# Two attention heads in the halves of the rows, four column blocks in the modulation, a copy before the norm

## The chip, the cores and the metric

The kernel runs on one core of a Trainium2 chip. The metric is the time of one execution in microseconds of the device, lower is better; the median of several runs is given. The core has five instruction streams: PE (TensorE, matmuls; its weight loads are a row of their own, PEld), DVE (VectorE), ACT (ScalarE), POOL (GpSimd) and SP (SyncE, which here only issues DMAs). Each works its instructions off in program order.

## The reference, cut to what matters

One even layer (mLSTM heads beside a Hyena channel group) and one odd layer (neighbourhood attention), each followed by an MLP; 1024 latent tokens, 256 context tokens, model width 1024, all in float32. Two parts of it matter here. Every layer first makes six vectors out of the conditioning vector, one for the latent tokens and one for the context tokens:

```python
mod_x = (silu_c @ w_mod[l] + b_mod[l])        # w_mod[l]: 1024 x 6144
mod_c = silu_cc @ w_mod[l] + b_mod[l]
```

And the odd layer's attention, 16 heads of width 64, where each latent query sees a window of 8 rows by 16 columns of the 16 x 64 token grid and all 256 context keys in one softmax:

```python
q = rms_norm(p[:, :, 0], qn) * NA_HD ** -0.5
k = rms_norm(p[:, :, 1], kn)
s_lat = jnp.einsum('bhqd,bhkd->bhqk', q_r, k_blk) + bias
s_ctx = jnp.einsum('bhqd,bhkd->bhqk', q_r, kc)
p = jax.nn.softmax(jnp.concatenate([s_lat, s_ctx], axis=-1), axis=-1)
out = p[..., :nk] @ v_blk + p[..., nk:] @ vc
```

## The kernel before

**Stages.** The program makes the Hyena filters (to some 230 us of the profile), the Hyena group (to 600), the mLSTM heads with the output projection (to 960), the first layer's MLP (to some 2000), the attention of the odd layer (2007 to 2650), its output projection and the second MLP. A scheduling layer sets each engine's order when the program is built: instructions have priorities (`pr`), work is taken in that order as its inputs and buffers come free, and what results is a fixed order for each engine.

**Matmuls in float32.** Where exactness matters, an operand is split into a high part of type F32R and the rest (`split`, L110: ACT casts, DVE or POOL subtracts, L112 and L113), and a product is the sum of three F32R matmuls: high by high, high by low, low by high (`gemm`, L177 to L179). An F32R matmul is one instruction in the profile. A plain F32 matmul is two, which are called passes here.

**The modulation** (`mod_steps`, L208). A third of a layer's w_mod (2048 columns) is worked off in 16 steps: a step loads 128 rows by 1024 columns (512 KB) into a tile `wm` and multiplies it by the conditioning vectors. The weights of the matmul are only 32 columns wide, so its output goes to one of four blocks of 32 partitions of one bank: step (k, jj) writes blocks 2jj and 2jj+1 with 512 columns each (L218). The first third of layer 0 is made at the start with three `wm` tiles (bank `psq`), the other two thirds during the mLSTM stage, up to four steps behind each load that `wload` makes (L162, bank `psn`), and the three of layer 1 during the first MLP, four steps for each pair of weight blocks, with a single `wm` tile (L296, bank `psm`): there a step's DMA is issued only when the matmuls of the step before it have read the tile.

**The attention** (`natten_proj`, L890; `natten_attn`, L946) works two heads at a time, eight times. The projection makes q and k of both heads in 128 rows (64 each), each group of up to 512 tokens in a bank `psg`, and normalises them from there: ACT squares the bank (L901), PE sums over each head's 64 rows (L903), ACT and DVE make the inverse root, and DVE multiplies the bank by it (L912, L914). Then the q of each head is written twice by ACT: `Q[hh]` holds the high part of head hh in both halves of its 128 rows (four 64-row copies per group, L933) and `Ql[hh]` the low part in one half and zeros in the other (L934, POOL clears it). `Kt[hh]` holds the high part of the head's k in one half and its low part in the other (L939, L940). So one matmul over 128 rows gives high by high plus high by low, and a second one, with `Ql`, low by high. For each of four blocks of query columns (cb), each head (hh) and each of two row blocks (rb) these two matmuls are made against the 256 context keys (into `pc`) and against a window of 384 keys (into `p_`), L979 and L980. Then come the row maximum (L983, L985), the exponentials (L990, L991), the scaling (L995), transposes on PE (L1000, L1007) that ACT and DVE copy out (L1002, L1009), and the products with the values (L1015, L1019), in which the two heads' outputs go to the two halves of the 128 partitions.

**Banks.** PSUM has eight banks, shared out by tag: `psum(**PS3)` (g=3, f=3, m=1, n=1) holds from the mLSTM stage to the end. The attention takes its projections from `g`, its scores and outputs from `f`, all transposes from `m`, the norm's sum from `n`. `PS2` is defined and not used.

Of the kernel before, what the change touches and what calls it, by code (L numbers as in the profile page):

```python
# [17 lines left out]
P = 128  # L18
# [9 lines left out]
def kernel(ctx: ExitStack, tc: tile.TileContext, A, out):  # L28
# [38 lines left out]
    PS2 = dict(g=3, f=3, m=1, q=1)  # L67
# [33 lines left out]
    def sub(o, a, b):  # L101
        return tt(o, a, b, ALU.subtract)
# [105 lines left out]
    def mod_steps(l, g, pool, bufs, tag):  # L208

        ps = [None]  # L210
        for i in range(16):
            def step(k=i // 2, jj=i % 2):
                if k == 0 and jj == 0:
                    ps[0] = pt([P, 512], tag)
                w = mk(pool, [P, 8, P], bufs[0], bufs[1]).rearrange("p a b -> p (a b)")
                nc.sync.dma_start(w, A["w_mod"][l, k * P:(k + 1) * P, g * 2048 + jj * 1024:g * 2048 + (jj + 1) * 1024])
                for j in (2 * jj, 2 * jj + 1):
                    T.matmul(ps[0][32 * j:32 * j + 32, :], sil[:, k, :], w[:, (j - 2 * jj) * 512:(j - 2 * jj + 1) * 512],  # L218
                             start=(k == 0), stop=(k == 7))
                if k == 7 and jj == 1:  # L220
                    mod_end(l, g, ps[0], tag)
            yield step
# [667 lines left out]
    def natten_proj(hp, h, ap_, nl, cst, order=((0, 0), (0, 1), (1, 0), (1, 1), (1, 2), (2, 0), (2, 1), (2, 2))):  # L890

        with pr("np"):
            bd, gain = cst

            Q = [mk(nl, [P, LAT], "Q", 4, F32R) for _ in range(2)]
            Ql = [mk(nl, [P, LAT], "Ql", 3, F32R) for _ in range(2)]
            for hh in range(2):
                G.memset(Ql[hh][64 - 64 * hh:128 - 64 * hh].bitcast(F32), 0.0)
            def normed(ps, n, sc):
# [20 lines left out]
            for j, g in order:  # L920
                t0, n = GR[g]
                if j not in w:
                    w[j] = wload("qkv" if hp else "q0", A["w_qkv"][3 * hp + j], E4 if hp == 0 else None, into=(nl, ("Q", "Q"), 4) if hp == 0 and j == WQ else None)
                ts = slice(t0, t0 + n)
                ps = gemm(w[j], h, g, n)
                if j == 0:
                    r = normed(ps, n, gain)
                    blkd = lambda x: x.rearrange("p (c r q) -> p c r q", c=4, q=16)
                    rv = r.rearrange("p (r c q) -> p c r q", c=4, q=16)
                    for hh in range(2):  # L930
                        a = slice(64 * hh, 64 * hh + 64)
                        for b in (0, 64):
                            S.copy(blkd(Q[hh][b:b + 64, ts]), rv[a])  # L933
                        sub(blkd(Ql[hh][a, ts]), rv[a], blkd(Q[hh][a, ts]).bitcast(F32))  # L934
                elif j == 1:
                    r = normed(ps, n, None)
                    for hh in range(2):
                        a, b = slice(64 * hh, 64 * hh + 64), slice(64 - 64 * hh, 128 - 64 * hh)
                        S.copy(Kt[hh][a, ts], r[a, :n])  # L939
                        sub(Kt[hh][b, ts], r[a, :n], Kt[hh][a, ts].bitcast(F32))  # L940
                else:
                    with pr("v0" if hp == 0 else None):
                        S.copy(vT[:, ts], ps[:, :n])
            return Q, Ql, Kt, vT

    def natten_attn(hp, qkv, ap_, nl, store):  # L946
        with pr("na"):
            Q, Ql, Kt, vT = qkv
# [12 lines left out]
            for cb in range(4):  # L961
# [4 lines left out]
                pT = []  # L966
                for hh in range(2):
                    TM = mk(nl, [P, 2, 384], "TM", 2)
                    nc.gpsimd.dma_start(TM, A["rpbT"][2 * hp + hh, ct])
                    kl = Kt[hh][:, 0:LAT].rearrange("p (r c) -> p r c", c=64)  # L970
                    pc = pt([P, 2, CTX], "f")
                    st = mk(ap_, [P, 8], "st", 6)
                    pw, pe = [], []
                    for rb in range(2):
                        c0 = rb * 512 + cb * P
                        p_ = pt([P, 512], "f")
                        for o, kx in ((pc[:, rb], Kt[hh][:, LAT:NT]),
                                      (p_[:, :384], kl[:, 4 * rb:4 * rb + 12, KC0[cb]:KC0[cb] + 32])):
                            T.matmul(o, Q[hh][:, c0:c0 + P], kx, start=True, stop=False)  # L979
                            T.matmul(o, Ql[hh][:, c0:c0 + P], kx, start=False, stop=True)  # L980
                        pw.append(p_)
                        pe.append(mk(ap_, [P, 640], "pe", 4))
                    V.tensor_reduce(out=st[:, 0:2], in_=pc, axis=AX.X, op=ALU.max)  # L983
                    for rb in range(2):
                        V.tensor_tensor_reduce(out=pe[rb][:, 0:384], in0=pw[rb][:, :384], in1=TM[:, rb], scale=1.0, scalar=st[:, rb:rb + 1],  # L985
                                               op0=ALU.add, op1=ALU.max, accum_out=st[:, 2 + rb:3 + rb])
# [198 lines left out]

    with tc.tile_pool(name="nl", bufs=1, reuse_waits="tile") as nl, \
# [29 lines left out]
        for d in range(8):  # L1216
            w = wload("ow1", A["w_o"][d][:, 0:7], E5, (0, 7))
            residual(xg, 1, 0, d, 0, gemm(w, h2, 0, 512, ks=range(7)), 512)
    with tc.tile_pool(name="xg1", bufs=1, reuse_waits="tile", side="right") as xp:
# [149 lines left out]
```

## Time and profile before

| | us |
|---|---|
| median of 3 runs | 3432.65 (3432.45 to 3433.51) |
| the profiled execution's own time | 3440.28 |
| its span, first to last instruction | 3438.5 |
| PE busy | 3288.0 |
| DVE busy | 2055.2 |
| ACT busy | 1209.4 |
| POOL busy | 350.3 |

All microseconds in what follows come from this one profiled execution, whose time lies 7.6 us (0.2%) above the median of the runs. A row of the timeline has a start, a length, the engine, the line, output<-inputs and a count; for PE the shape `128*64 128x512` means 128 rows by 64 columns of weights and 512 moving columns. The length of a matmul contains a tail that overlaps the next one: what a matmul costs PE is the distance to the next start.

### The profile page before, as it was taken

How to read it: one execution, taken by the hardware profiler on the slowest of the kernel's cores; microseconds unless marked ns; L12 is line 12 of the kernel's file. 1: busy time of each engine (PE TensorE's matmuls, PEld its weight loads, DVE VectorE, ACT ScalarE, POOL GpSimd, SP SyncE). 2: the span in 40 equal slices, each digit the busy share in tenths (PEclk: the TensorE clock that was granted, in tenths of full speed). 3: DMA queues.
4: the chain of work that ended last, by engine and by line, in shares of the span. 5: the costliest groups of instructions: out<-in, count | busy, mean ns of one | idle time of the engine just before them, and what ended most of it. 6: DMA issues, size and time to landing. Idle time of an engine off the chain costs nothing.

```text
span 3438.5 us, 44541 instructions
## 1 busy us (share of the span) xinstructions
PE 3288.0 (96%) x17660; PEld 2647.1 (77%) x17660; DVE 2055.2 (60%) x3655; ACT 1209.4 (35%) x2554; POOL 350.3 (10%) x295
## 2 busy tenths in 40 slices
PE   6889979999999999999999999999999899999999
PEld 3777878677877878787788867777777688888887
DVE  4858978356576544444454676666676654545444
ACT  5742222244343121111212376666665421121211
POOL 1331222101121000000000121111110200000000
PEclk9999989999999999999999999999999999999999
DMA  6432221775632121222211112222225211111111
GB/s 202 156 108 67 79 63 58 239 230 198 209 131 81 55 92 56 82 66 68 68 36 45 68 54 67 68 68 67 62 70 169 74 50 49 48 45 49 49 49 68
DMA packets 104011, 306.07 MB, mean 89 GB/s; under 512 B 12497, under 2 KB 24905, under 8 KB 102394
## 3 DMA queue, kind: packets, MB, share of 16 engines
q1 hardware_dynamic: 94154, 266.60, 23.6%
q0 software_dynamic: 6464, 28.84, 2.8%
q10 hardware_dynamic: 3184, 7.78, 0.7%
q8 instruction: 139, 2.28, 0.3%
q14 instruction: 70, 0.57, 0.1%
HBM read 255.93 MB, written 43.05 MB: 87 GB/s over the span
## 4 chain that ended last, share of the span: by engine, by line
PE 76%; DVE 12%; DMA 5%; ACT 3%; POOL 3%; issue 2%; SPq 0%; ACTq 0%; DVEq 0%; POOLq 0%
PE psg L178 12%; PE psg L179 12%; PE psg L177 12%; PE psf L313 7%; PE psf L314 7%; PE psf L315 7%; DMA wm<-in_w_mod 2%; DVE b L96 2%; PE psf L1015 2%; DVE n L108 2%; PE psm L1000 1%; DVE q L96 1%; PE psm L218 1%; PE psf L979 1%; PE psf L980 1%
## 5 line engine op out<-in xcount | busy, mean ns | idle before, releaser
L177 PE MATMUL psg<-h,wh 128*128 128x512 f32 (+1 forms) x2728 | 1017.7, 373 | 20.0 <-ACT wh L112 9.4
L178 PE MATMUL psg<-h,wh 128*128 128x512 f32 (+1 forms) x2728 | 1017.1, 373 | 4.1 <-DVE h L108 2.8
L179 PE MATMUL psg<-h,wl 128*128 128x512 f32 (+1 forms) x2728 | 1008.8, 370 | 10.1 <-DVE wl L113 5.0
L177 PEld LDWEIGHTS psg<-h,wh 128*128 128x128 f32 x2728 | 519.4, 190 | 121.1 <-issue 22.2
L178 PEld LDWEIGHTS psg<-h,wh 128*128 128x128 f32 x2728 | 519.7, 191 | 120.6 <-issue 33.8
L179 PEld LDWEIGHTS psg<-h,wl 128*128 128x128 f32 x2728 | 519.0, 190 | 107.5 <-issue 17.3
L108 DVE SCALAR_TENSOR_TENSOR x<-psf,modT,x 128x512 f32<-128x512 f32 (+1 forms) x512 | 347.4, 683 | 223.0 <-PE psf L315 222.7
L314 PE MATMUL psf<-al,w2h 128*128 128x512 f32 (+1 forms) x1280 | 472.1, 369 | 0.5 <-DVE al L113 0.5
L315 PE MATMUL psf<-ah,w2l 128*128 128x512 f32 (+1 forms) x1280 | 471.5, 368 | 0.0
L313 PE MATMUL psf<-ah,w2h 128*128 128x512 f32 (+1 forms) x1280 | 469.5, 369 | 1.2 <-ACT ah L112 0.8
L112 ACT CAST w2h<-w2r 128x1024 fp32r<-128x1024 f32 x64 | 67.2, 1051 | 767.6 <-PE psf L314 596.0
L313 PEld LDWEIGHTS psf<-ah,w2h 128*128 128x128 f32 x1280 | 240.7, 189 | 45.4 <-ACT ah L112 3.8
L314 PEld LDWEIGHTS psf<-al,w2h 128*128 128x128 f32 x1280 | 241.6, 189 | 42.9 <-DVE al L113 1.8
L315 PEld LDWEIGHTS psf<-ah,w2l 128*128 128x128 f32 x1280 | 241.5, 189 | 41.2 <-issue 1.3
L112 ACT CAST wh<-wr 128x1024 fp32r<-128x1024 f32 (+2 forms) x144 | 148.5, 1031 | 292.7 <-PE psg L178 228.2
L113 DVE TENSOR_TENSOR wl<-wr,wh 128x1024 fp32r<-128x1024 f32 (+1 forms) x105 | 127.6, 1216 | 151.7 <-ACT wh L112 151.1
L108 DVE SCALAR_TENSOR_TENSOR rr<-psg,rr 128x512 f32<-128x512 f32 x160 | 101.4, 634 | 191.0 <-ACT rr L302 190.9
L113 POOL TENSOR_TENSOR wl<-wr,wh 128x1024 fp32r<-128x1024 f32 (+1 forms) x39 | 128.3, 3289 | 623.5 <-ACT wh L112 602.6
L113 DVE TENSOR_TENSOR w2l<-w2r,w2h 128x1024 fp32r<-128x1024 f32 x64 | 78.2, 1223 | 154.4 <-ACT w2h L112 152.6
L302 ACT ACTIVATE rr<-psg 128x512 f32<-128x512 f32 x160 | 88.1, 551 | 212.5 <-PE psg L179 211.1
L112 ACT CAST ah<-rr 128x512 fp32r<-128x512 f32 x160 | 92.3, 578 | 164.1 <-DVE rr L108 164.1
L113 DVE TENSOR_TENSOR al<-rr,ah 128x512 fp32r<-128x512 f32 x160 | 101.8, 636 | 77.6 <-ACT ah L112 77.6
(294 smaller groups left out, 4353.5 us busy)
## 6 DMA issues: line engine op xcount, KB each, us to landing
wm<-in_w_mod SPq DMA_DIRECT2D x96, 512.0 KB
wr<-in_w SPq DMA_DIRECT2D x64, 512.0 KB
w2r<-in_w SPq DMA_DIRECT2D x64, 512.0 KB
big<-d SPq DMA_DIRECT2D x39, 640.0 KB
TM<-in_rpbT POOLq DMA_DIRECT2D x64, 384.0 KB, 3.4
wr<-in_w_in SPq DMA_DIRECT2D x29, 512.0 KB
wr<-in_w_qkv SPq DMA_DIRECT2D x24, 512.0 KB
d<-b SPq DMA_DIRECT2D x8, 1280.0 KB
```

Of the source, the lines that this page charges most:

```text
L96: return (e or V).tensor_tensor(out=o, in0=a, in1=b, op=op)
L108: return V.scalar_tensor_tensor(out=o, in0=a, scalar=s, in1=b, op0=op0, op1=op1)
L112: S.copy(hi, x)
L113: (e or V).tensor_tensor(out=lo, in0=x, in1=hi.bitcast(F32), op=ALU.subtract)
L177: T.matmul(ps[:M, :n], hi[:, k, :M], hh[g][:, k, :n], start=(i == 0), stop=False)
L178: T.matmul(ps[:M, :n], hi[:, k, :M], hl[g][:, k, :n], start=False, stop=False)
L179: T.matmul(ps[:M, :n], lo[:, k, :M], hh[g][:, k, :n], start=False, stop=(i == len(ks) - 1))
L302: S.activation(r[:, :n], ps[:, :n], AF.Relu)
L313: T.matmul(ps[:, :n], w2h[:, d], ah[g], start=(i == 0), stop=False)
L314: T.matmul(ps[:, :n], w2h[:, d], al[g], start=False, stop=False)
L315: T.matmul(ps[:, :n], w2l[:, d], ah[g], start=False, stop=(i == 1))
L1015: T.matmul(po[64 * hh:64 * hh + 64, rb], Vw[:, rb + j, 64 * hh:64 * hh + 64], pT[hh][0][rb][:, j], start=(j == 0), stop=False)
```

## The change

Three parts, and the numbers of tiles and banks that go with them.

**Scores.** `Q[0]` and `Kt[0]` now hold the high parts of both heads, `Q[1]` and `Kt[1]` the low parts: one `split` for each group in place of the copies by halves, and no `Ql`. The three products of a head are matmuls over its own 64 rows, written alternately for head 0 (rows 0 to 63 of the array) and head 1 (rows 64 to 127), each head into a bank of its own. Both heads' scores are now made before either head's softmax.

**Projection.** Before the norm of q and k, ACT copies the bank into a tile `qs`; the square and the last multiplication read the copy.

**Modulation.** A step now loads 256 of each of four 512-column blocks (128 rows by 4 runs of 1 KB instead of one run of 4 KB), and writes all four blocks of 32 partitions with 256 columns each. The 16 steps go through the eight k for the first 256 columns, then for the second 256.

**Banks.** `PS2` becomes g=2, f=4, m=1, n=1 and holds during the attention; `PS3` is set again behind it. `TM` has three tiles instead of two, `pe` six instead of four.

```diff
-    PS2 = dict(g=3, f=3, m=1, q=1)
+    PS2 = dict(g=2, f=4, m=1, n=1)
...
-            def step(k=i // 2, jj=i % 2):
-                if k == 0 and jj == 0:
+            def step(k=i % 8, c0=i // 8 * 256):
+                if k == 0 and c0 == 0:
                     ps[0] = pt([P, 512], tag)
-                w = mk(pool, [P, 8, P], bufs[0], bufs[1]).rearrange("p a b -> p (a b)")
-                nc.sync.dma_start(w, A["w_mod"][l, k * P:(k + 1) * P, g * 2048 + jj * 1024:g * 2048 + (jj + 1) * 1024])
-                for j in (2 * jj, 2 * jj + 1):
-                    T.matmul(ps[0][32 * j:32 * j + 32, :], sil[:, k, :], w[:, (j - 2 * jj) * 512:(j - 2 * jj + 1) * 512],
-                             start=(k == 0), stop=(k == 7))
+                w = mk(pool, [P, 8, P], bufs[0], bufs[1]).rearrange("p (j a) b -> p j (a b)", j=4)
+                nc.sync.dma_start(w, A["w_mod"][l, k * P:(k + 1) * P, g * 2048:(g + 1) * 2048].rearrange("p (j c) -> p j c", j=4)[:, :, c0:c0 + 256])
+                for j in range(4):
+                    T.matmul(ps[0][32 * j:32 * j + 32, c0:c0 + 256], sil[:, k, :], w[:, j], start=(k == 0), stop=(k == 7))
...
-            def normed(ps, n, sc):
+            def normed(pj, n, sc):
+                ps = mk(nl, [P, 512], "qs", 2)
+                S.copy(ps[:, :n], pj[:, :n])
...
-                    for hh in range(2):
-                        a = slice(64 * hh, 64 * hh + 64)
-                        for b in (0, 64):
-                            S.copy(blkd(Q[hh][b:b + 64, ts]), rv[a])
-                        sub(blkd(Ql[hh][a, ts]), rv[a], blkd(Q[hh][a, ts]).bitcast(F32))
+                    split(blkd(Q[0][:, ts]), blkd(Q[1][:, ts]), rv)
...
-                    for hh in range(2):
-                        a, b = slice(64 * hh, 64 * hh + 64), slice(64 - 64 * hh, 128 - 64 * hh)
-                        S.copy(Kt[hh][a, ts], r[a, :n])
-                        sub(Kt[hh][b, ts], r[a, :n], Kt[hh][a, ts].bitcast(F32))
+                    split(Kt[0][:, ts], Kt[1][:, ts], r[:, :n])
...
-                            T.matmul(o, Q[hh][:, c0:c0 + P], kx, start=True, stop=False)
-                            T.matmul(o, Ql[hh][:, c0:c0 + P], kx, start=False, stop=True)
...
+                def scores(outs, rb, cols):
+
+                    c0 = rb * 512 + cb * P
+                    for i, (x, y) in enumerate(((0, 0), (0, 1), (1, 0))):
+                        for hh in range(2):
+                            T.matmul(outs[hh], Q[x][HD[hh], c0:c0 + P], cols(Kt[y])[HD[hh]], start=(i == 0), stop=(i == 2))
...
+    psum(**PS2)
     with tc.tile_pool(name="nl", bufs=1, reuse_waits="tile") as nl, \
...
+    psum(**PS3)
     with tc.tile_pool(name="xg1", bufs=1, reuse_waits="tile", side="right") as xp:
```

The order on PE in the attention, before: one column block of one of the last heads. `psg` rows are the projection of the next pair of heads, `psm` the transposes, `KK` and `Q`, `Ql` the scores.

```order
L1000 MATMUL psm_17837<-ident,pe_17818 128x128 x3
L1015 MATMUL psf_17897<-s_3172_17835,Vw_17801 64x128
L979 MATMUL psf_17932<-KK_17349,Q_17343 128x256
L980 MATMUL psf_17932<-KK_17349,Ql_17345 128x256
L979 MATMUL psf_17932<-KK_17349,Q_17343 128x256
L980 MATMUL psf_17932<-KK_17349,Ql_17345 128x256
L177 MATMUL psg_18234<-h_1652_8689,wh_18186 128x512
L178 MATMUL psg_18234<-h_1653_8690,wh_18186 128x512
L1007 MATMUL psm_17843<-ident,pe_17812 128x128 x2
L1007 MATMUL psm_17843<-ident,pe_17818 128x128 x2
L979 MATMUL psf_17934<-KK_17349,Q_17343 128x384
L980 MATMUL psf_17934<-KK_17349,Ql_17345 128x384
```

The scores stand among projections and transposes, all of which use the whole array. The same place in the changed program, the context keys first (`psf_18192` is head 0, `psf_18193` head 1; `KK_17589` and `Q_17587` are the high parts):

```order
L1015 MATMUL psf_18149<-s_3188_18106,Vw_18045 64x128
L971 MATMUL psf_18192<-KK_17589,Q_17587 128x256
L971 MATMUL psf_18193<-KK_17589,Q_17587 128x256
L971 MATMUL psf_18192<-KK_17590,Q_17587 128x256
L971 MATMUL psf_18193<-KK_17590,Q_17587 128x256
L971 MATMUL psf_18192<-KK_17589,Q_17588 128x256
L971 MATMUL psf_18193<-KK_17589,Q_17588 128x256
L1007 MATMUL psm_18114<-ident,pe_18050 128x128 x2
L1007 MATMUL psm_18114<-ident,pe_18051 128x128 x2
L971 MATMUL psf_18192<-KK_17589,Q_17587 128x256
```

and a few rows on, the window keys of the first row block (`psf_18208` is head 0, `psf_18209` head 1):

```order
L971 MATMUL psf_18208<-KK_17589,Q_17587 128x384
L1000 MATMUL psm_18130<-ident,pe_18055 128x128 x3
L971 MATMUL psf_18208<-KK_17590,Q_17587 128x384
L971 MATMUL psf_18208<-KK_17589,Q_17588 128x384
L900 MATMUL psn_18483<-n_3273_18481,bd_8340 128x512
L1000 MATMUL psm_18136<-ident,pe_18056 128x128 x3
L1015 MATMUL psf_18149<-s_3194_18134,Vw_18045 64x128
```

For the context keys the two heads alternate, as written. For these window keys they don't: head 0's three matmuls come first, with transposes among them, and head 1's three only after the next products with the values. Over the whole attention 542 of the 768 score matmuls stand next to one of the other head, and 226 do not, 215 of them 384 wide.

The modulation on PE in the first MLP, one step among the projections (`psg`), before:

```order
L179 MATMUL psg_10008<-h_1543_8262,wl_9999 128x512
L177 MATMUL psg_10008<-h_1543_8262,wh_9998 128x512
L218 MATMUL psm_8695<-wm_9972,sil 32x512 x2
L178 MATMUL psg_10008<-h_1544_8263,wh_9998 128x512
L179 MATMUL psg_10008<-h_1543_8262,wl_9999 128x512
```

and in the changed program:

```order
L179 MATMUL psg_13617<-h_1543_8358,wl_13608 128x512
L177 MATMUL psg_13617<-h_1543_8358,wh_13607 128x512
L218 MATMUL psm_12272<-wm_13575,sil 32x256 x4
L178 MATMUL psg_13617<-h_1544_8359,wh_13607 128x512
L179 MATMUL psg_13617<-h_1543_8358,wl_13608 128x512
```

Each step has four narrower matmuls in the place of two, and in the first MLP the same 16 projection matmuls stand between the steps of a group of four as before. In the mLSTM stage the 32 steps make 37 blocks among other work instead of 34, since seven of them are split, one matmul here and three a little later.

More of the change, by code (lines that the diff above doesn't have):

```diff
@@ L895, in natten_proj @@
             Q = [mk(nl, [P, LAT], "Q", 4, F32R) for _ in range(2)]
-            Ql = [mk(nl, [P, LAT], "Ql", 3, F32R) for _ in range(2)]
-            for hh in range(2):
-                G.memset(Ql[hh][64 - 64 * hh:128 - 64 * hh].bitcast(F32), 0.0)
-            def normed(ps, n, sc):
+            def normed(pj, n, sc):
+                ps = mk(nl, [P, 512], "qs", 2)
+                S.copy(ps[:, :n], pj[:, :n])
                 sq = n2()
@@ L943, in natten_proj @@
                         S.copy(vT[:, ts], ps[:, :n])
-            return Q, Ql, Kt, vT
+            return Q, Kt, vT
     def natten_attn(hp, qkv, ap_, nl, store):
         with pr("na"):
-            Q, Ql, Kt, vT = qkv
+            Q, Kt, vT = qkv
             vl = vT[:, 0:LAT].rearrange("p (r c) -> p r c", c=64)
@@ L966, in natten_attn @@
                 pT = []
+                HD = [slice(64 * hh, 64 * hh + 64) for hh in range(2)]
+                TMs, sts, pes = [], [], []
                 for hh in range(2):
-                    TM = mk(nl, [P, 2, 384], "TM", 2)
+                    TM = mk(nl, [P, 2, 384], "TM", 3)
                     nc.gpsimd.dma_start(TM, A["rpbT"][2 * hp + hh, ct])
-                    kl = Kt[hh][:, 0:LAT].rearrange("p (r c) -> p r c", c=64)
-                    pc = pt([P, 2, CTX], "f")
-                    st = mk(ap_, [P, 8], "st", 6)
@@ L973, in natten_attn @@
[L973 to L986, printed above, removed]
+                    TMs.append(TM)
+                    sts.append(mk(ap_, [P, 8], "st", 6))
+                    pes.append([mk(ap_, [P, 640], "pe", 6) for _ in range(2)])
@@ new lines, in scores @@
+                def scores(outs, rb, cols):
[3 more added lines that the diff above has]
+                            T.matmul(outs[hh], Q[x][HD[hh], c0:c0 + P], cols(Kt[y])[HD[hh]], start=(i == 0), stop=(i == 2))
+                pcs = [pt([P, 2, CTX], "f") for _ in range(2)]
+                for rb in range(2):
+                    scores([x[:, rb] for x in pcs], rb, lambda k: k[:, LAT:NT])
@@ new lines, in natten_attn @@
+                for hh in range(2):
+                    V.tensor_reduce(out=sts[hh][:, 0:2], in_=pcs[hh], axis=AX.X, op=ALU.max)
+                for rb in range(2):
+                    pw = [pt([P, 512], "f") for _ in range(2)]
+                    scores([x[:, :384] for x in pw], rb,
+                           lambda k: k[:, 0:LAT].rearrange("p (r c) -> p r c", c=64)[:, 4 * rb:4 * rb + 12, KC0[cb]:KC0[cb] + 32])
+                    for hh in range(2):
+                        V.tensor_tensor_reduce(out=pes[hh][rb][:, 0:384], in0=pw[hh][:, :384], in1=TMs[hh][:, rb], scale=1.0,
+                                               scalar=sts[hh][:, rb:rb + 1], op0=ALU.add, op1=ALU.max, accum_out=sts[hh][:, 2 + rb:3 + rb])
@@ L987, in natten_attn @@
+                for hh in range(2):
+                    st, pe, pc = sts[hh], pes[hh], pcs[hh]
                     V.tensor_scalar(out=st[:, 2:4], in0=st[:, 2:4], scalar1=-1.0, scalar2=None, op0=ALU.mult)
```

3 lines of the change are left out of this document (1 added, 2 removed).

## The prediction

> **What bounds the kernel now.** First the page: its totals and the engines of the chain that ended last.
>
> ```profile
> span 3438.5 us, 44541 instructions
> PE 3288.0 (96%) x17660; PEld 2647.1 (77%) x17660; DVE 2055.2 (60%) x3655; ACT 1209.4 (35%) x2554; POOL 350.3 (10%) x295
> PE 76%; DVE 12%; DMA 5%; ACT 3%; POOL 3%; issue 2%; SPq 0%; ACTq 0%; DVEq 0%; POOLq 0%
> ```
>
> PE is nearly always busy and carries 76% of the chain. So I ask of each edit what it does to the distance from one matmul's start to the next. The windows of the four stages that it touches (columns: window, length, busy of PE, PEld, DVE, ACT, POOL, granted clock, DMA share, GB/s): the start, the mLSTM stage, the first MLP, the attention.
>
> ```profile
> 0.00:55.00 55.00, 31.42 (x104) 8.09 (x104) 16.60 (x40) 20.44 (x40) 1.63 (x9) 0.88 0.75 247
> 600.00:800.00 200.00, 192.75 (x1052) 137.94 (x1052) 90.45 (x216) 67.20 (x200) 19.62 (x8) 0.98 0.69 228
> 1050.00:1710.00 660.00, 655.81 (x3333) 521.22 (x3332) 304.99 (x463) 122.63 (x193) 3.50 (x4) 1.00 0.24 74
> 2007.00:2650.00 643.00, 630.47 (x4147) 493.05 (x4147) 447.36 (x998) 424.15 (x1051) 88.25 (x134) 0.99 0.25 76
> ```
>
> PE stands still for 7.3 of 200, 4.2 of 660 and 12.5 of 643 us in the last three; work taken from PE there, or given to it, shows in the time. At the start PE idles 23.6 of 55 us and the DMAs move 247 GB/s.
>
> **The modulation.** One step in the first MLP, with the projections around it, and two steps of the mLSTM stage which the scheduler had torn apart:
>
> ```profile
> 1088.04 1.05 PE L218 MATMUL psm<-wm,sil 128*32 128x512 f32 x4
> 1089.03 0.50 PE L178 MATMUL psg<-h,wh 128*128 128x512 f32 x1
> 1089.36 0.40 PE L179 MATMUL psg<-h,wl 128*128 128x512 f32 x1
> 1089.60 0.39 PE L177 MATMUL psg<-h,wh 128*128 128x512 f32 x1
> ...
> 1092.56 0.39 PE L178 MATMUL psg<-h,wh 128*128 128x512 f32 x1
> 1093.06 1.05 PE L218 MATMUL psm<-wm,sil 128*32 128x512 f32 x4
> ```
>
> ```profile
> 646.93 1.04 PE L218 MATMUL psn<-wm,sil 128*32 128x512 f32 x2
> 647.90 0.66 PE L785 MATMUL psm<-ident,big 128*128 128x128 f32 x4
> 648.49 1.06 PE L218 MATMUL psn<-wm,sil 128*32 128x512 f32 x6
> 649.48 0.50 PE L178 MATMUL psg<-h,wh 128*128 128x512 f32 x1
> ```
>
> A block of two instructions (one matmul) holds PE for 0.97 us (646.93 to 647.90), one of four (two matmuls, a whole step) 0.99 (1088.04 to 1089.03), one of six 0.99 (648.49 to 649.48). So matmuls for different blocks of 32 partitions run side by side, three at least, and a block costs its two passes whatever its width in blocks. Four at once is what the change needs; I take it as given. Within the block of two, the second starts 0.45 us after the first (the row lasts 1.04, one instruction 0.59, by the least in the next rows). A pass over 512 columns so costs at most 0.45, and half the columns save some 0.21 of each: 0.99 becomes 0.57, a gain of 0.42 for each step.
>
> ```profile
> L218 PE MATMUL psm<-wm,sil x192: 592/605/617, 1050.9 to 1700.8; 128*32 128x512 f32 x192
> L218 PE MATMUL psn<-wm,sil x128: 592/617/1062, 615.3 to 797.7; 128*32 128x512 f32 x128
> L218 PE MATMUL psq<-wm,sil x64: 592/825/1063, 11.3 to 48.4; 128*32 128x512 f32 x64
> 1089.14 3.88 DMA wm<-in_w_mod
> 2664.86 3.86 DMA wr<-in_w_o
> ```
>
> At four instructions a step these are 48, 32 and 16 steps (the last two rows are of the chain of waits: start, length, DMA). First MLP: 48 x 0.42 = 20.2 us. But there the next step's DMA is issued only once the tile is read (1089.14), lands 3.88 us later, and PE arrives about then: 1092.56 to 1093.06 is 0.50 where 0.23 is usual (1089.36 to 1089.60). Both the DMA's issue and PE's return move forward by the same amount, so the wait only grows if the load takes longer in runs of 1 KB. The nearest row is the load of 2664.86, 512 KB in runs of 512 bytes: 3.86 us, no longer. I take 0.1 us for 36 of the 48 steps (three in each four follow closely), 3.6 us, with ends of 0 and 0.3 (11 us). That leaves 16.6. mLSTM stage: 32 x 0.42 = 13.4, less two or three blocks more than before at 0.57 (torn steps) and the 7.3 us in which PE waits anyway: 10, with ends of 6 and 13. Start: matmuls at 825 against 605 ns, three tiles in turn, so each round of load and matmul gets shorter by part of a step, and the loads have more pieces: 3, with ends of -3 and 6. Sum: 29.6 us less.
>
> **The scores.** One stretch of the attention:
>
> ```profile
> L1015 PE MATMUL psf<-s,Vw x768: 272/273/476, 2048.2 to 2651.6; 128*64 128x128 f32 x192
> 2151.20 0.55 PE L1000 MATMUL psm<-ident,pe 128*128 128x128 f32 x3 [0.19 <-ACT s L1002]
> 2151.68 0.43 PE L1015 MATMUL psf<-s,Vw 128*64 128x128 f32 x2
> 2152.05 0.39 PE L979 MATMUL psf<-KK,Q 128*128 128x256 f32 x1
> 2152.27 0.28 PE L980 MATMUL psf<-KK,Ql 128*128 128x256 f32 x1
> 2152.39 0.28 PE L979 MATMUL psf<-KK,Q 128*128 128x256 f32 x1
> 2152.51 0.28 PE L980 MATMUL psf<-KK,Ql 128*128 128x256 f32 x1
> ...
> 2153.09 0.60 PE L1007 MATMUL psm<-ident,pe 128*128 128x128 f32 x4
> ...
> 2153.71 0.34 PE L980 MATMUL psf<-KK,Ql 128*128 128x384 f32 x1
> 2153.89 0.40 PE L178 MATMUL psg<-h,wh 128*128 128x512 f32 x1
> ```
>
> A score matmul costs 0.12 us at 256 columns (2152.39 to 2152.51) and 0.18 at 384 (2153.71 to 2153.89). Before there are 256 of each: 30.7 + 46.1 = 76.8 us. The change has 384 of each, with 64 rows. If two heads that stand next to each other run side by side, the 256-wide ones take some 192 slots and the 384-wide ones, 169 in pairs and 215 alone by the order, some 300: 23.0 + 54.0 = 77.0. So even then the matmuls gain nothing: the three products cost in halves what two cost in full, and torn pairs eat the rest. If none run side by side it is 115.2, 38 us more.
>
> Then there is the price of changing the array's partition. L1015 and L1019 use it in halves of columns. The row of three L1000 starts its last at 2151.48 (0.55 less 0.27, the length of one); L1015 follows 0.20 later where 128 columns take 0.11 (four L1007 in 0.60), and its second pass 0.16 later (0.43 less 0.27): 0.14 us lost on entering. It then leaves at 2152.05, 0.21 after that second pass, and the next start is 0.22 on where 0.12 is usual: 0.20 lost. By the order there are 192 such changes before and 476 after, counted from the last modulation step to the end, since almost each short run of half-row matmuls stands between full ones: 284 more. The bounds are 0.10 each (only the drain, where the weights of the next would wait for a semaphore anyway) and 0.17 (half of 0.34): 28 and 48 us. I take the middle, 0.13: 37 us. The nearest row with halves of rows is one from the gates, F32 and without a partner:
>
> ```profile
> 235.63 0.28 PE L178 MATMUL psg<-h,wh 128*128 128x256 f32 x1
> 235.86 1.10 PE L675 MATMUL psg<-s,q 64*100 64x512 f32 x2
> ```
>
> It starts 0.23 after a matmul that takes 0.12: 0.11 lost on entering. The Trainium skill, TensorEngine Tiling, section Tiling Modes, speaks against this change with the same rule: "Changing tiling mode (not just tile) drains the TensorE". It gives no price; by it all 284 changes cost, as in the sum.
>
> **The copy, the casts, the banks.**
>
> ```profile
> L933 ACT CAST Q<-n 64x512 fp32r<-64x512 f32 x64 | 39.5, 618 | 0.8
> L957 ACT COPY Vw<-psm 128x512 f32<-128x512 f32 x32 | 18.6, 582 | 7.3 <-PE psm L955 7.3
> L96 DVE TENSOR_TENSOR Ql<-n,Q 64x512 fp32r<-64x512 f32 x32 | 21.8, 681 | 2.9 <-ACT Q L933 2.5
> L96 DVE TENSOR_TENSOR KK<-n,KK 64x512 fp32r<-64x512 f32 x32 | 22.0, 686 | 1.9 <-ACT KK L939 0.9
> ```
>
> For a q group ACT drops from four casts to one and gains a copy (0.58, by the copy of the same size): 16 groups x (3 x 0.62 - 0.58) = 20 us less; for k one cast goes and the copy comes, even. DVE loses half of its 64-row subtractions: 22 us. ACT and DVE have idle time in this stage (424 and 447 of 643), so this buys time only by ending PE's waits sooner. The copy lies ahead of the square and lengthens the norm's chain by 0.58 for a pair of heads' group; projections for the next pair run a whole pair ahead, which hides it; if that cover were gone it would be 40 x 0.58 = 23 us. Two `g` banks instead of three suffice if the copy comes within a gemm's length (24 matmuls x 0.23 = 5.5 us). PE's idle 12.5 us shrink when PE itself becomes slower, its helpers lighter and `f` deeper: I take 10 off, with ends of 0 and 12.5. POOL no longer clears `Ql`; nothing waits for that.
>
> **The sum.** Modulation -29.6, score matmuls 0, changes of partition +37, waits -10: -2.6 us. Against its own time of 3440.28 the profiled execution would come to 3437.7; against the median of 3432.65, which lies 7.6 below, 3430. A difference under 0.2% (6.9 us, 3425.8 to 3439.5) is about what a measurement of this kernel cannot tell from none. With its bounds this case reaches from 3412 (changes at 0.10, full gains) to 3455 (0.17, waits kept, late loads).
>
> **The rivals.**
>
> *Free changes.* Matmuls in F32R may enter and leave a part of the array without a drain. For it speaks the only F32R row with half an array:
>
> ```profile
> 231.23 0.28 PE L178 MATMUL psg<-h,wh 128*128 128x256 f32 x1
> 231.35 1.09 PE L671 MATMUL psg<-h,wh 128*64 128x512 f32 x4
> ```
>
> 64 columns of weights after 128, and it starts 0.12 us later, as always. Against it: that matmul has no partner in the other half, so it may not use a divided array at all. The 284 changes then cost nothing: -29.6 - 10 = -40, 3393. Chance 0.17.
>
> *Free, but one after the other.* If F32R matmuls don't divide the array, halves don't overlap either: +38, no changes, -10 of waits, -29.6: -2, 3431. Chance 0.13.
>
> *One after the other, and each change paid*: slower. No row shows two F32R matmuls side by side; the pairs that are seen to overlap are F32. Then +38 + 37 - 12 - 29.6 = +33, 3466. It decides as soon as fewer than a third of the pairs overlap. Against it: the column blocks overlap so cleanly. The Trainium skill, TensorE: Matmul & The Clock Gate, Part 3, says that matmuls in different row groups run concurrently, measured 3.07 times faster for four; no run here shows it, and by it the score matmuls cost the 77 us of the sum. Chance 0.13.
>
> *Late modulation loads.* Four times as many pieces take 0.6 us longer in 36 steps: +18 against the forecast, 3448. Against it stands the 3.86 us of 512-byte runs. Chance 0.07.
>
> **How the numbers follow.** The forecast's case has 0.50, the rivals 0.17, 0.13, 0.13, 0.07. Range 3393 to 3462: it takes in the forecast's case, the second and fourth rival and about half of each of the others, so some 0.15 is left out. Faster by over 0.2%: 0.17 from the first rival, 0.17 of the forecast's 0.50, 0.05 of the second: 0.39. Slower: 0.15 of the forecast's, 0.13, 0.06, 0.02: 0.36. Within: 0.25.
>
> **What would show it.** In the profile after, a modulation block should hold PE for 0.57 us, with PE's wait ahead of it in the MLP up by 0.1. Two score matmuls of different heads should start within hundredths of a microsecond, with the next pair 0.12 or 0.18 on. The first matmul after a run of half rows should come 0.1 late, and the one after it 0.1 more. The window from the first to the second MLP should be some 27 us longer, the first MLP 17 shorter. The forecast is wrong if L971 enters without delay (then 3393), if pairs start a slot apart (then 3466), or if blocks of four still hold PE for 0.9 us (then +25).

## The result, and the profile after

The changed kernel takes 3477.38 us (median of 4 runs, 3475.41 to 3479.45) against 3433.08 for the kernel before (4 runs, 3432.45 to 3436.87): 44 us or 1.2% slower, ratio 1.0123 with an interval of 1.011 to 1.0136. The forecast was 3430, the range ended at 3462. The two profiled executions took 3479.45 and 3440.28 us, 39.2 apart, which is what has to be explained below.

The page of the changed kernel: totals, and the engines of the chain that ended last.

```profile
span 3477.7 us, 45667 instructions
PE 3305.4 (95%) x18300; PEld 2656.4 (76%) x18300; DVE 2030.0 (58%) x3615; ACT 1189.5 (34%) x2523; POOL 340.6 (10%) x279
PE 64%; DVE 4%; DMA 3%; ACT 2%; issue 1%; POOL 1%; SPq 0%; ACTq 0%; DVEq 0%; POOLq 0%
```

DVE and ACT are busy for 25 and 20 us less and the program is 39 us longer: as in the kernel before, PE sets the time. So the question is again where the distance between the starts of PE's matmuls grew.

**Before the attention the change gains.** One modulation step of the first MLP (the projections around it are L177 to L179), and two groups of L218 (in each row the last two times are the first and the last start of the group):

```profile
1080.02 0.39 PE L177 MATMUL psg<-h,wh 128*128 128x512 f32 x1
1080.70 0.64 PE L218 MATMUL psm<-wm,sil 128*32 128x256 f32 x8 [0.29 <-DMA wm<-in_w_mod]
1081.27 0.50 PE L178 MATMUL psg<-h,wh 128*128 128x512 f32 x1
...
L218 PE MATMUL psm<-wm,sil x384: 379/391/403, 1039.8 to 1675.9; 128*32 128x256 f32 x192
...
L218 PE MATMUL psq<-wm,sil x128: 379/634/637, 11.4 to 44.4; 128*32 128x256 f32 x128
```

The eight instructions (four matmuls of two passes) hold PE from 1080.70 to 1081.27: 0.57 us where a step took 0.99. The wait ahead of it for the DMA is in brackets. The first step ends at 44.4 instead of 48.4, the last of the first MLP starts at 1675.9 instead of 1700.8.

**Behind it, it loses more.** For one stretch of the program I take one of the last matmuls of the first MLP and one of the first output matmuls of the second MLP. Line numbers moved by one between the kernels, so L314 is not the same matmul in both; the neighbours are 0.1 to 0.2 us apart. The kernel before, then the changed one:

```profile
1975.49 0.28 PE L314 MATMUL psf<-al,w2h 128*128 128x256 f32 x1
...
2743.38 0.39 PE L314 MATMUL psf<-al,w2h 128*128 128x512 f32 x1
```

```profile
1950.49 0.28 PE L314 MATMUL psf<-ah,w2l 128*128 128x256 f32 x1
...
2783.06 0.39 PE L314 MATMUL psf<-ah,w2l 128*128 128x512 f32 x1
```

The stretch begins 25.0 us earlier and lasts 832.6 instead of 767.9 us, 64.7 longer; the second MLP takes the same time in both. 64.7 less 25.0 is 39.7, less some half a microsecond behind it the 39.2 of the two executions.

The 64.7 us can be split, since on PE every start follows another. This is my own count over all matmul records of the two traces, not a view of the profile. For each pair of neighbouring starts in the stretch I count the usual distance of the first one's kind as work (0.227, 0.177, 0.120, 0.109 us for 512, 384, 256, 128 columns, 0.43 for a plain F32 matmul of 512; among the halves of a divided array the distance that there is). At a change of the array's partition up to 0.095 of what is left is a drain. What is left behind the first matmul of a new partition is its weight load in the open. The rest is a wait where the trace names a releaser.

| us of PE in this stretch | before | changed |
|---|---|---|
| all matmuls but the scores | 602.4 | 602.8 |
| score matmuls | 76.0 | 77.5 |
| drains (192 changes before, 476 now) | 18.0 | 44.3 |
| behind the first matmul of a partition | 12.9 | 42.5 |
| waits for another engine | 36.4 | 45.2 |
| irregular distances without a releaser | 22.3 | 20.5 |

The changes of partition went from 30.9 to 86.8 us: 55.9 for 284 changes, 0.197 each. The waits rose by 8.8. One run of half rows shows how a change is paid (timeline of PE in the changed kernel):

```profile
2137.85 0.66 PE L945 MATMUL psm<-ident,vs 128*128 128x128 f32 x4
2138.43 0.80 PE L971 MATMUL psf<-KK,Q 64*128 64x384 f32 x6
2139.16 0.50 PE L179 MATMUL psg<-h,wl 128*128 128x512 f32 x1
2139.50 0.40 PE L177 MATMUL psg<-h,wh 128*128 128x512 f32 x1
2139.74 0.39 PE L178 MATMUL psg<-h,wh 128*128 128x512 f32 x1
```

The six score matmuls are three pairs: the two of a pair start 0.003 us apart, so they do run side by side, and three slots of 0.177 should take 0.53. They hold PE for 0.73 (2138.43 to 2139.16). By the single instructions behind this row, 0.10 is lost behind the first pair, whose successors' weights are not loaded yet, and 0.09 at the end in the drain. The full matmul behind it pays the same 0.11 once more (2139.16 to 2139.50 is 0.34, then 0.24 and less). The weight loads at that place show what happens:

```profile
2139.16 0.19 PEld L179 LDWEIGHTS psg<-h,wl 128*128 128x128 f32 x1 [0.26 <-issue]
2139.27 0.19 PEld L177 LDWEIGHTS psg<-h,wh 128*128 128x128 f32 x1
2139.50 0.19 PEld L178 LDWEIGHTS psg<-h,wh 128*128 128x128 f32 x1
2139.74 0.19 PEld L179 LDWEIGHTS psg<-h,wl 128*128 128x128 f32 x1
```

The loads for the second, third and fourth matmul start at 2139.27, 2139.50 and 2139.74. From the third on, each starts together with the matmul ahead of it (2139.50, 2139.74) and is hidden behind it. The second starts 0.11 after the first matmul (2139.16), because the first load was not made ahead of time, and its matmul comes 0.11 late. The Trainium skill, TensorEngine Tiling (Array Packing), Key Properties, speaks of a drain at a change of mode; the trace agrees, 0.09 us, but that is only half the price here.

The largest new wait is a single one, at the start of the stretch (timeline of PE in the changed kernel):

```profile
1969.97 1.19 PE L266 MATMUL psm<-s,ones 128*128 128x256 f32 x2 [19.20 <-DVE s L96]
1971.79 0.80 PE L177 MATMUL psg<-h,wh 128*128 128x512 f32 x1 [0.62 <-ACT n L130]
1972.38 0.63 PE L178 MATMUL psg<-h,wh 128*128 128x512 f32 x1
1972.81 0.63 PE L179 MATMUL psg<-h,wl 128*128 128x512 f32 x1
...
1974.94 0.44 PE L178 MATMUL psg<-h,wh 128*128 128x512 f32 x1
```

PE stands for 19.2 us until the sum for the norm of the context tokens is there, and only then begins the first projection of the attention. The same matmul in the kernel before:

```profile
1995.86 1.22 PE L267 MATMUL psm<-s,ones 128*128 128x256 f32 x2 [3.15 <-DVE s L96]
```

In both kernels it starts some 20 us after the last matmul of the first MLP (1975.61 before, 1950.49 now). But before, it stood behind 66 matmuls of the projections, which filled that time, and PE waited 3.2 us for it. After the long wait the matmuls come 0.43 us apart for 3 us instead of 0.23. Three windows there (changed kernel, changed kernel, kernel before; third column from the right: the granted clock) show why:

```profile
1972.00:1975.00 3.00, 3.00 (x8) 2.32 (x9) 2.23 (x4) 0.75 (x3) 0.92 (x2) 0.50 0.00 0
1975.00:1978.00 3.00, 3.00 (x15) 2.44 (x14) 2.96 (x7) 2.96 (x7) 1.64 (x2) 1.00 0.00 0
...
1995.30:1998.70 3.40, 2.84 (x7) 2.29 (x8) 0.59 (x3) 1.30 (x3) 0.00 (x0) 0.50 0.00 0
```

The clock is at half, and it was so in the kernel before too, behind its 3.2 us. So most of what is new at this place is the wait itself.

### The profile page after: what moved, and what is told of

The parts are those of the page before. It is cut to its first block, busy times and chain, and to the rows that moved or that the text cites. A ratio compares the mean times of both kernels' runs of the same rounds, so it can differ in the third digit from the quotient of the medians.

```text
span 3477.7 us, 45667 instructions
## 1 busy us (share of the span) xinstructions
PE 3305.4 (95%) x18300; PEld 2656.4 (76%) x18300; DVE 2030.0 (58%) x3615; ACT 1189.5 (34%) x2523; POOL 340.6 (10%) x279
## 4 chain that ended last, share of the span: by engine, by line
PE 64%; DVE 4%; DMA 3%; ACT 2%; issue 1%; POOL 1%; SPq 0%; ACTq 0%; DVEq 0%; POOLq 0%
PE psg L177 10%; PE psg L179 10%; PE psg L178 10%; PE psf L312 7%; PE psf L313 7%; PE psf L314 7%; PE psf L971 3%; PE psf L1015 2%; PE psm L1000 2%; DMA wm<-in_w_mod 1%; DVE n L108 1%; PE psn L900 1%; PE psm L1007 1%; PE psf L1019 1%; PE psm L218 1%; DMA wr<-in_w_o 1%
## 5 line engine op out<-in xcount | busy, mean ns | idle before, releaser
L177 PE MATMUL psg<-h,wh 128*128 128x512 f32 (+1 forms) x2728 | 1015.9, 373 | 18.6 <-ACT h L289 8.4
L179 PE MATMUL psg<-h,wl 128*128 128x512 f32 (+1 forms) x2728 | 1011.6, 371 | 13.2 <-DVE wl L113 7.1
L177 PEld LDWEIGHTS psg<-h,wh 128*128 128x128 f32 x2728 | 518.3, 190 | 121.5 <-issue 22.4
L179 PEld LDWEIGHTS psg<-h,wl 128*128 128x128 f32 x2728 | 518.5, 190 | 113.6 <-issue 18.1
L314 PE MATMUL psf<-ah,w2l 128*128 128x512 f32 (+1 forms) x1280 | 472.2, 369 | 0.0
L313 PEld LDWEIGHTS psf<-al,w2h 128*128 128x128 f32 x1280 | 241.8, 189 | 42.5 <-DVE al L113 2.0
L314 PEld LDWEIGHTS psf<-ah,w2l 128*128 128x128 f32 x1280 | 241.9, 189 | 40.8 <-issue 0.9
L113 POOL TENSOR_TENSOR wl<-wr,wh 128x1024 fp32r<-128x1024 f32 (+1 forms) x39 | 138.2, 3543 | 604.3 <-ACT wh L112 604.3
```

Of the source, the lines that this page charges most:

```text
L113: (e or V).tensor_tensor(out=lo, in0=x, in1=hi.bitcast(F32), op=ALU.subtract)
L177: T.matmul(ps[:M, :n], hi[:, k, :M], hh[g][:, k, :n], start=(i == 0), stop=False)
L179: T.matmul(ps[:M, :n], lo[:, k, :M], hh[g][:, k, :n], start=False, stop=(i == len(ks) - 1))
L313: T.matmul(ps[:, :n], w2h[:, d], al[g], start=False, stop=False)
L314: T.matmul(ps[:, :n], w2l[:, d], ah[g], start=False, stop=(i == 1))
```

## The experiments

All times stand against runs of the kernel before that were taken alongside (their medians were 3435.8 to 3439.7 us), as a ratio with its interval. There are three sets, taken on different chips, and the result above is a fourth; where two runs of different sets are compared, the text says so, and such a difference carries both intervals.

**The modulation alone** (L208 as changed, all else as before), timed twice, the second time with more runs.

```diff
-            def step(k=i // 2, jj=i % 2):
+            def step(k=i % 8, c0=i // 8 * 256):
...
```

> The four-block modulation alone, all else as before. Theory: its gain and the loss in the attention add up, since in the changed kernel's trace the first MLP ends 25.0 us earlier and all behind that is longer; so 25 us less than before, 3408, with 48 blocks of the first MLP at 0.57-0.58 us and a wait ahead of them that is longer by some 4 us in all. Rival 1: the late loads are a property of the changed schedule, then the 29.6 us of the prediction, 3403. Rival 2: the gain is given back behind the MLP (the attention's start is held by something else than PE), then 3425 or more.

> The four-block modulation alone once more, in five rounds, since its first timing (18 us less than before, interval 14 to 26) and its trace (26 us less) differ. Theory: the trace's 25 us, 0.9927 of the time before. Rival: 18 us, 0.9948.

Measured: 0.9942 (0.9925 to 0.9959), then 0.9936 (0.9923 to 0.9949), so 22 us less with 18 to 26 in the second. The two matmuls that bound the stretch, in the trace of the second timing:

```profile
1954.44 0.28 PE L314 MATMUL psf<-ah,w2l 128*128 128x256 f32 x1
...
2719.06 0.39 PE L314 MATMUL psf<-ah,w2l 128*128 128x512 f32 x1
```

The first MLP ends 21.1 us earlier than before, 24.8 in the first run's trace; the stretch behind it keeps its 764.6 us (767.1 in the first run, 767.9 before). So the gain is kept to the end: rival 2 falls. The interval of the second timing holds the theory's 25 us, and it does not exclude the 18 of the first timing; the 29.6 of the prediction lie outside both intervals. This kernel is the fastest of all that ran.

**All but the modulation.**

```diff
-            def step(k=i % 8, c0=i // 8 * 256):
+            def step(k=i // 2, jj=i % 2):
...
```

> The changed kernel with the old modulation: scores in halves of the rows, the copy, the new banks. Theory: the two parts are independent, then before plus the 64.7 us by which the stretch from the first MLP's last matmul to the second's first grew: 3498. Rival: the modulation's earlier end disturbs what follows (the 19 us wait of PE at the start of the attention exists only with it), then 3479.

Measured: 1.0187 (1.0168 to 1.0206), 65 us more. The stretch lasts 829.2 us and PE's wait for the norm's sum is there as well, 19.2 us. The two parts add up; the rival falls.

**The price of a change of partition by itself.** Kernel before, with the second of each two score matmuls on 64 rows:

```diff
-                            T.matmul(o, Ql[hh][:, c0:c0 + P], kx, start=False, stop=True)
+                            hs = slice(64 * hh, 64 * hh + 64)
+                            T.matmul(o, Ql[hh][hs, c0:c0 + P], kx[hs], start=False, stop=True)
```

> The kernel before, but the second score matmul of each pair uses only the 64 rows in which its low parts are not zero. Same products, same widths, no partner in the other half: only the 64-row shape is new. By the order there are 687 changes of the array's partition instead of 192, 495 more, and the score matmuls take the same 76.0 us of slots. Theory: each change costs 0.18 to 0.20 us (a drain of 0.09 and a weight load in the open of 0.10), so 89 to 99 us more, 3522 to 3532. Rival 1: the 0.13 of the prediction, 64 us, 3497. Rival 2: in F32R a change costs nothing without a partner in the other half, 3433.

Measured: 1.0252 (1.0235 to 1.0269), 87 us more for 495 changes, 0.175 each in the time. PE's timeline in this kernel, four score matmuls of 256 columns in turn over 128 and 64 rows:

```profile
2149.82 0.38 PE L979 MATMUL psf<-KK,Q 128*128 128x256 f32 x1
2150.14 0.38 PE L981 MATMUL psf<-KK,Ql 64*128 64x256 f32 x1
2150.45 0.39 PE L979 MATMUL psf<-KK,Q 128*128 128x256 f32 x1
2150.76 0.38 PE L981 MATMUL psf<-KK,Ql 64*128 64x256 f32 x1
2151.07 0.50 PE L177 MATMUL psg<-h,wh 128*128 128x512 f32 x1
```

Each start comes 0.31 after the last where 0.12 is usual: 0.19 for every change, although nothing runs in the other half of the array. By the split above drains rose from 18.0 to 64.9 and what lies behind first matmuls from 12.9 to 65.2, 0.200 for each of the 495; the waits fell by 6.6. Both rivals fall: a change in F32R is neither free nor worth 0.13.

**The sharing of the banks one norm earlier.** The changed kernel, in which the banks are shared out anew ahead of the context tokens' norm:

```diff
         def after(g, t0, n):
+            if g == 2:
+                psum(**PS2)
...
-    psum(**PS2)
     with tc.tile_pool(name="nl", bufs=1, reuse_waits="tile") as nl, \
```

> The changed kernel, but the banks are shared out anew one norm earlier, ahead of the norm of the context tokens instead of behind it, so that this norm's matmul no longer has to stand ahead of all projections. Theory: the 20.0 us that PE waits there for the norm's sum (4.0 in the kernel before) come from the place of the new sharing; they fall to about 4, so some 16 us less than the changed kernel, 3461. Rival: PE waits there because the projections themselves are not ready, or loses the same time a little later; then 3477.

Measured: 1.009 (1.0075 to 1.0105), 31 us above the kernel before; the changed kernel's 1.0123 is from another set, so the gain is some 11 us and not sharply known. PE's waits from the end of the first MLP on:

```profile
engine line waited for: us in total, times, longest us
PE psg L177 <- ACT vT L933: 7.3, 1, 7.3
PE psm L1000 <- ACT s L1002: 1.1, 2, 0.6
```

The 19.2 us are gone, so the place of the new sharing was their cause: a matmul that uses the old sharing has to stand ahead of all that use the new one. But 7.3 us come back: a projection finds both `g` banks taken until ACT copies one out (L933 at 1972.33), and that copy stands behind the squares of the context tokens' norm in ACT's order (L250, the last from 1971.09). By the split the waits fall by 11.1, from 45.2 to 34.1. The theory was right on the cause and missed the second wait.

**The banks alone**, on the kernel before (two banks for projections, four for scores, shared out at the places of the changed kernel, no copy), and **the kernel with the earlier sharing, without the copy**:

```diff
-    PS2 = dict(g=3, f=3, m=1, q=1)
+    PS2 = dict(g=2, f=4, m=1, n=1)
...
+    psum(**PS2)
     with tc.tile_pool(name="nl", bufs=1, reuse_waits="tile") as nl, \
...
+    psum(**PS3)
     with tc.tile_pool(name="xg1", bufs=1, reuse_waits="tile", side="right") as xp:
```

> The kernel before, with the banks of the attention shared out as in the changed kernel (two for projections, four for scores) and at the same places; scores, copy and modulation as before. Theory: the wait at the start of the attention comes from the new sharing alone, 16 us more than before, and the third bank of the projections is missed at the start (7 us): together 16 to 23 us more. Rival: four banks for the scores end other waits, and it comes out within 5 us of before.

```diff
-                ps = mk(nl, [P, 512], "qs", 2)
-                S.copy(ps[:, :n], pj[:, :n])
+                ps = pj
```

> The kernel with the earlier sharing of the banks, without the copy ahead of the norm: the norm reads the projection's bank as it did before. By the order there are 474 changes of partition instead of 476, and the slots of the scores are 76.1 us. Theory: the copy is what makes two banks suffice; without it a bank is held through the whole norm, and PE waits for banks, 10 to 40 us more than with the copy. Rival: the copy is only ACT's work beside PE's, and the time stays within 3 us.

Measured: the banks alone 1.0161 (1.0143 to 1.0179), 55 us more; without the copy 1.0143 (1.0128 to 1.0158), 18 us above the 1.009 of the run with it (another set). PE's waits, banks alone:

```profile
PE psm L267 <- DVE s L96: 19.9, 1, 19.9
PE psg L177 <- DVE n L96: 15.5, 9, 2.0
PE psn L903 <- ACT n L901: 11.2, 7, 1.7
```

and without the copy:

```profile
PE psm L999 <- ACT s L1001: 6.6, 9, 0.8
PE psn L899 <- ACT n L897: 6.2, 8, 3.4
PE psg L177 <- DVE n L96: 2.0, 2, 1.5
```

The long wait belongs to the sharing alone. With two banks nine projections wait for the norm to let go of one (15.5 us), and seven of the norm's sums wait for the squares that ACT makes ahead of them (11.2). In the changed kernel, with the copy, neither is among the waits above 0.2 us. So the copy pays for the third bank: part of what the change spends buys back what another part of it took away. Both rivals fall, and the banks alone cost over twice what I expected. But taking out the copy brings back only 2.0 us of waiting for a bank. Beside the 7.3 us, which are there with and without it, most of the waiting is for the norm's squares (6.2) and in the transposes (6.6 where the copy left 1.1). So the theory on the copy held for the time and not for the wait that it named; why those other waits grow is not shown.

**Both heads' score banks in one tile**, so that their matmuls become ready together, on the kernel with the earlier sharing:

```diff
-                pcs = [pt([P, 2, CTX], "f") for _ in range(2)]
+                pj = pt([P, 2, 2, CTX], "f")
+                pcs = [pj[:, hh] for hh in range(2)]
...
-                    pw = [pt([P, 512], "f") for _ in range(2)]
+                    pwj = pt([P, 2, 512], "f")
+                    pw = [pwj[:, hh] for hh in range(2)]
...
```

The outputs' tile takes two banks as well, and `f` has two such tiles in place of four banks.

> The kernel with the earlier sharing of the banks (the run before it), but the score banks of the two heads are one tile of two banks, so that both heads' matmuls become ready together. By the order 740 of the 768 score matmuls now stand in pairs (542 before), their slots fall from 77.0 to 58.7 us, and the changes of partition from 476 to 422. Theory: 18 us of slots and 54 x 0.20 = 11 us of changes are gained, 29 us, which brings it from 33 us above the kernel before to about 4 above. Rival: with two double tiles in the place of four banks, PE waits for the row maxima to free them, and most of the 29 us comes back as waits for DVE.

Measured: 1.0035 (1.0022 to 1.0049), 12 us above the kernel before, and 19 below the 1.009 of the run with the earlier sharing (another set), where the theory had 29. By the split the scores fall by 18.0 us, to 59.5, drains and weight loads by 6.5, and the waits rise by 7.3, the largest new group seven waits for `pe` from DVE, 7.1 us together. The rival's waits for the row maxima are only 1.3 us (L971 <- DVE st). So the halves are worth their 18 us once nothing tears the pairs apart, and it is still not enough: 422 changes cost more than before by 48 us.

**Fewer changes in the kernel that was left.** The products with the values (L1015, L1019) make the 192 changes of the kernel before. On the modulation alone, in two steps: all products of a column block in one piece, or in two.

```diff
-                for rb in range(2):
-                    for j in range(3):
-                        for hh in range(2):
+                for rb in (1, 0):
+                    for j in (1, 0):
+                        for hh in (1, 0):
...
```

> The kernel before with the four-block modulation, and the products with the values written in the reverse order, so that the first of them needs the operand that is ready last: the 20 of one column block then stand in one piece, and there are 64 changes of partition instead of 192 by the order. Nothing else is changed. Theory: 128 changes less at 0.16 (the 30.9 us that the 192 cost in the trace of before) to 0.20: 20 to 26 us less than the modulation alone, so some 38 to 51 us less than the kernel before. Rival: the wait for the last operand is now in one piece on PE, and the scheduler has nothing to put there; then no more than 5 us less than the modulation alone.

```diff
-                        for hh in range(2):
+                        for hh in (1, 0):
```

> The kernel before with the four-block modulation, and in the products with the values head 1 ahead of head 0 in each pair, whose operands come later: by the order the products of one column block stand in two pieces instead of three (a single product no longer runs ahead of its partner), 128 changes of partition instead of 192, and no piece waits for the last operand of all. Theory: 64 x 0.16 to 0.20 = 10 to 13 us less than the modulation alone in the same call. Rival: as with all 20 products in one piece, buffers held longer put waits on PE and lower its clock, and it is slower than the modulation alone.

Measured: in one piece 1.0117 (1.0101 to 1.0133), 40 us above before and 60 above the 0.9942 of the modulation alone (another set); in two pieces 1.0021 (1.0011 to 1.003), against 0.9936 for the modulation alone in the same set, so 29 us lost. By the split the changes became cheaper, about as expected in one piece and by more in two: drains, weight loads and the products themselves fall by 22.1 and by 16.4 us. But the waits rise, in one piece from 37.3 to 90.1 us, in two from 35.3 to 65.5, and irregular distances from 21.9 to 56.2 and from 21.4 to 36.1. A slower clock fits the irregular distances: between 2007 and 2650 us the granted clock is 0.91 in one piece and 0.97 in two, against 1.00 with the modulation alone. PE's timeline at the turn from one pair of heads to the next, in one piece, and windows there (granted clock in the third column from the right):

```profile
2167.68 0.34 PE L979 MATMUL psf<-KK,Ql 128*128 128x384 f32 x1
2169.82 0.39 PE L978 MATMUL psf<-KK,Q 128*128 128x256 f32 x1 [1.81 <-DVE st L984]
...
2170.85 0.52 PE L979 MATMUL psf<-KK,Ql 128*128 128x384 f32 x1
2173.01 0.69 PE L978 MATMUL psf<-KK,Q 128*128 128x384 f32 x1 [1.64 <-DVE st L984]
...
2177.95 0.90 PE L999 MATMUL psm<-ident,pe 128*128 128x128 f32 x3 [1.07 <-ACT s L1001]
```

```profile
2166.00:2170.00 4.00, 2.19 (x19) 1.70 (x14) 2.24 (x5) 0.96 (x2) 1.62 (x2) 1.00 0.49 161
2170.00:2174.00 4.00, 2.36 (x8) 1.36 (x8) 3.66 (x10) 2.68 (x9) 0.56 (x1) 0.54 0.33 100
2174.00:2178.00 4.00, 2.88 (x7) 1.06 (x6) 2.93 (x8) 1.80 (x5) 1.43 (x2) 0.50 0.32 98
2178.00:2182.00 4.00, 4.00 (x13) 3.38 (x14) 0.93 (x3) 3.59 (x11) 0.00 (x0) 0.50 0.00 0
2182.00:2186.00 4.00, 4.00 (x17) 3.03 (x16) 3.82 (x7) 1.45 (x5) 0.00 (x0) 0.76 0.01 4
```

At each turn of the pairs PE now waits twice for a score bank, 1.8 and 1.6 us here, and then has no projections left to put in between; for some 14 us behind that its clock is at half. That these turns run dry because the projections were spent earlier, in the places that the products left, is argued, not shown. Three of PE's waits in the attention, two in one piece and one in two pieces:

```profile
PE psf L978 <- DVE st L984: 28.0, 16, 2.0
PE psf L1014 <- DVE pc L1008: 7.0, 9, 0.8
...
PE psn L902 <- ACT n L900: 11.9, 11, 1.7
```

Both rivals were right that these kernels are slower than the modulation alone, but only in part on the reason. In one piece the longest row is the wait for score banks (28.0 us), and the products wait 7.0 us for an operand. In two pieces the longest row is the norm's sums waiting for ACT (11.9 us). So a new order that saves changes of partition cost more than it saved; the second rival's lower clock is shown, its buffers that are held longer are not.

## Why the prediction was wrong

The profiled execution was to come out 2.6 us shorter and came out 39.2 longer. By its steps:

**The modulation, -29.6: nearly right.** Blocks of four hold PE for 0.57, as worked out. In the first MLP the blocks fell from 48.1 to 27.9 us and the waits ahead of them rose from 4.4 to 8.4, 16.2 less where 16.6 was said; in the mLSTM stage the blocks fell by 12.0 and the waits rose by 1.6, 10.4 less for 10; the start's last step is 4.0 earlier for 3. Some of it is lost on the way: the end of the first MLP is 25.0 us earlier, and the modulation alone measures 22.

**The score matmuls, 0: right.** 76.0 became 77.5. Pairs do run side by side, and the torn ones eat the rest; with the pairs kept together it is 59.5.

**The changes of partition, +37: mechanism right, price too low.** The 284 extra changes are those that the order shows; each costs 0.197 us and not 0.13, 55.9 in all, beyond even the upper bound of 0.17. I took 0.13 as a middle between a drain alone (0.10) and half of the 0.34 that one run of products with the values loses. But the rows already shown gave both halves of the price, 0.1 for the drain and 0.1 for a weight load in the open, and the prediction's own last part says so (a first matmul 0.1 late, the next 0.1 more); the sum did not use it. The supposition that the weights would wait for a semaphore anyway was wrong for rows: in the 64-row experiment the waits fell by only 6.6 us beside 99 us of changes.

**The waits, -10: failed.** The small waits did shrink, from 32.4 to 25.2 us without the one at the start, by 7. But the one at the start grew from some 4 to 20.0 (3.2 and 19.2 for the norm's sum alone). It lies ahead of 2007 us, where the window of the prediction's 12.5 us of idle time began. The prediction asked whether two banks suffice and not what a new sharing does to the order at its seam: in the sequence of PE the context tokens' norm had moved from behind 66 projection matmuls to ahead of all of them, which the order of the changed program shows.

Both failed terms together are 38 us: 19 for the price and 19 for the waits. With the modulation's 4.6 us (25.0 for 29.6) that is nearly all of the 41.8 us between forecast and trace. None of the rivals was it. The one that named a slower time, one after the other and each change paid, had the wrong mechanism, since the pairs overlap; that also ends the rival of free changes one after the other. Free changes and late loads are ruled out by the 64-row experiment and by the waits of the first MLP (4.0 us more, where the forecast had 3.6 and that rival 18 on top).

## What to carry to other kernels

Before you divide the array for some of the matmuls, count in the order how often the partition changes, and price each change at a drain plus one weight load in the open, here 0.2 us: short runs among full matmuls lose more than the halves gain. A new sharing of PSUM banks in mid program is a seam: look which instructions of the old sharing must now stand ahead of all of the new one, and test the parts of a change one by one, since here a gain of 22 us lay in it beside a loss of 65. A wait of PE can cost its length and a stretch at half clock behind it.

## What the runs showed of the hardware

A matmul over half the rows pays the full change of partition in F32R even when nothing runs in the other half (0.19 us, four times in a row, above). Two F32R matmuls in the halves of the rows start 0.003 us apart.

The clock of PE can fall after short waits. In the kernel with all products in one piece 1.81 us of idleness are followed within a microsecond by a granted clock of 0.54 and 0.50, and it takes until about 2184 to come back, some 14 us, in which PE waited again for 1.64 and 1.07. In the changed kernel the 19.2 us wait is followed by 3 us at half speed. The Trainium skill, TensorE: Matmul & The Clock Gate, section Why this matters for your kernels, advises against PE-idle gaps above some 3 us between bursts; the second case agrees, the first shows that less can do it.

The stretches at half clock have steps. The traces have the clock at half from 1995.3 to 1998.7 us in the kernel before, from 2170.3 to 2184.0 in one piece, and from 1954.5 to 1975.0 in the changed kernel: 3.4, 13.7 and 20.5 us, which is one, four and six times 3.41.
